# The norms of two products: a root with one Newton step, two column pairs at once, no adding DMA

## The chip, the cores and the metric

One core of one Trainium2 chip. The time is the device time of one execution in microseconds; the profile is of one execution, recorded by the hardware profiler. PE is TensorE's matmuls, PEld its weight loads, DVE is VectorE, ACT ScalarE, POOL GpSimd, SP the engine that only issues transfers.

## The reference

Two networks behind each other on an activation of 256 positions by 1024 channels, all in f32. The first block, with `T = 256` positions:

```
u = rms_norm(h, norm_mix_pre);  proj = u @ w_in            # 1024 x 6656
four branches of width 256 (LRU, pooling, HGRN, short conv), each @ its w_branch, gated, summed = merged
h = h + rms_norm(merged @ w_out, norm_mix_post)            # 1024 x 1024
u = rms_norm(h, norm_mlp_pre);  hid = relu(u @ w_up)**2    # 1024 x 4096
h = h + rms_norm(hid @ w_down, norm_mlp_post)              # 4096 x 1024
rms_norm(x, g) = x * rsqrt(mean(x*x) + 1e-6) * g
```

The second block has two layers. Each is a gated feed-forward net (`ffn1`: norm, 1024 x 5632, silu(a)*b, 2816 x 1024), a mixer (projections `qkv`, `glu`, `gat`; q and k normalised and turned with rope tables; windowed attention, a convolution of 31 taps, products `att`, `cpr` and `out`), a second such net (`ffn2`) and a norm. The output is the activation after both layers.

## The kernel before

The activation stands transposed: channels on the 128 partitions, 256 positions along the free dimension, so a product of 1024 inputs has eight input slices `k`, and its outputs come in column pairs of 256 channels, one PSUM bank per pair (three banks `mm` take turns). For f32 accuracy each weight block (128 x 2048, 1 MB) and each input is split into a high part (`hi`, a ScalarE cast to the matmul's type) and a low part (`lo`, the weight less its high part, on VectorE), and each pair is the sum of three products per slice and half: high by high, high by low, low by high; 48 matmuls for a pair of eight slices.

`weights` (line 159) serves the blocks in a planned order, `ahead` blocks before their use: SP issues the transfer into one of two `raw` buffers, ScalarE casts `hi`, VectorE subtracts `lo`; `hi` and `lo` have three buffers each. Where the plan says `how=1`, ScalarE writes the block's negative, rounded to the matmul's type, into `lo` instead (line 180), and a transfer of POOL's queue adds the block from memory to it as it lands (line 181); the plan of block 1 does this for pairs 1 and 3 of `wout` (line 746).

The order of the instructions of each engine is set before the run by a scheduler: among what is ready by its own model, it takes what the program wrote first; `high_priority(offset=300)` counts its instructions as if written 300 earlier, and `issue_after(ins)` puts what it holds behind `ins` on that engine. So a position in the code is not a position in a queue.

`post` (line 922) does `w_out` and `w_down` with their norms. Over four pairs, each result is squared (ScalarE) and added up, and scaled by its gain into `post`. For the last pair, TensorE adds the squares over the channels with a column of ones (`colsum`, line 258; 256 sums, two columns of 128), VectorE makes the inverse root of these 128 x 2 numbers in eleven steps (`rsqrt`, line 241: affine, a first guess by the bits, three Newton steps of three), and TensorE spreads it over the partitions (`bcast`, line 282). Then, pair by pair, VectorE multiplies and adds to the residual (lines 948 and 949), and `norm.feed` (line 328) splits the new activation, scaled by the next norm's gain, into the next product's inputs `xs` (cast on ScalarE, line 301; low part on VectorE, line 302). The next norm's own factor is applied after the next product (`norm.done`, line 348), so that product can start with the first slice. `post` holds the weights back: in its last pair only one block is fetched ahead (`hold`), and the low part of the block after that is put behind the last feed (`issue_after`).

The next product after `w_out` is `wup` (line 909), that after `w_down` is `ffn1` of layer 0 (lines 370 and 376): pair by pair with `mm` (line 225).

The mixer (line 409) begins with two rope tables per layer: SP issues a small transfer `qkg` (line 425) and POOL makes eight products of it (line 430). They depend on nothing else than free tiles.

## Time and profile before

| | us |
|---|---|
| median of three runs (lowest, highest) | 1859.76 (1857.1, 1862.05) |
| the profiled execution | 1860.85 |
| its span, first to last instruction | 1859.1 |
| PE busy in it | 1789.8 |
| DVE busy | 1329.3 |
| ACT busy | 922.5 |
| POOL busy | 45.1 |

The mean granted clock of TensorE is 0.987 of its full speed. A busy time tells how long an engine had an instruction in work, not that it was at its best; the time that can be had is where TensorE waits or where its clock is low. The span is that of the profiled execution; the time of an execution is some 1.75 us longer than its span.

### The profile page before, as it was taken

The numbers are of one execution on the slowest core, as the hardware profiler recorded it, in microseconds if no ns is written. First come the engines' busy times: TensorE is split into PE (matmuls) and PEld (weight loads), VectorE is DVE, ScalarE is ACT, GpSimd is POOL, SyncE is SP. The second block draws the span as 40 slices with busy tenths as digits, with TensorE's granted clock in tenths as the row PEclk, the third lists the DMA queues.
The fourth block names the chain that finished last, engine by engine and source line by source line (L and its number), as shares of the span: only waits on it lengthen the run. The fifth ranks groups of instructions, "written<-read, shape, count | busy, mean of one in ns | idle before, by whom it ended". The sixth has DMA issues, their size and how long they took to land.

```text
span 1859.1 us, 32925 instructions
## 1 busy us (share of the span) xinstructions
PE 1789.8 (96%) x14048; PEld 1708.5 (92%) x14048; DVE 1329.3 (72%) x2047; ACT 922.5 (50%) x1036; POOL 45.1 (2%) x71
## 2 busy tenths in 40 slices
PE   8999989998999999989999999999999989999997
PEld 7989989997999997778999999999997778999997
DVE  7985777545765698888776656765599888776653
ACT  4354544333544455566654445444454566654442
POOL 0000000000000000000010000000000000000000
PEclk9999989999999999999999999999999999999999
DMA  7526645553555568886355555555569886355552
GB/s 284 175 98 204 186 149 188 182 182 122 204 182 185 179 205 268 235 249 181 129 198 182 182 180 183 182 182 193 180 197 267 257 237 181 128 191 182 184 185 85
DMA packets 53858, 350.57 MB, mean 189 GB/s; under 512 B 6224, under 2 KB 6352, under 8 KB 14288
## 3 DMA queue, kind: packets, MB, share of 16 engines
q1 hardware_dynamic: 47664, 309.44, 47.0%
q0 software_dynamic: 5184, 37.75, 10.7%
q8 instruction: 110, 1.80, 0.4%
q10 hardware_dynamic: 864, 1.28, 0.2%
q14 instruction: 36, 0.29, 0.0%
HBM read 347.40 MB, written 1.05 MB: 187 GB/s over the span
## 4 chain that ended last, share of the span: by engine, by line
PE 66%; issue 14%; DMA 10%; DVE 6%; ACT 4%; POOL 0%; ACTq 0%; DVEq 0%; POOLq 0%
PE mm L222 60%; DMA raw<-qkv 7%; ACT hi L182 3%; DMA raw<-gat 2%; DVE lo L184 2%; PE y L552 1%; PE tr L544 1%; PE pc L264 1%; PE pc L274 1%; PE sc L527 1%; DMA raw<-out 1%; DMA lo<-wout 0%; PE pb L286 0%; DVE spare L589 0%; PE sc L531 0%
## 5 line engine op out<-in xcount | busy, mean ns | idle before, releaser
L222 PE MATMUL mm<-xs,hi 128*128 128x256 f32 x5568 | 1003.7, 284 | 10.5 <-ACT hi L173 5.9
L222 PEld LDWEIGHTS mm<-xs,hi 128*128 128x128 f32 x5568 | 853.1, 190 | 18.7 <-ACT hi L173 5.9
L184 DVE TENSOR_TENSOR lo<-raw,hi 128x2048 fp32r<-128x2048 f32 (+1 forms) x252 | 569.2, 2259 | 308.2 <-ACT hi L182 307.8
L222 PE MATMUL mm<-xs,lo 128*128 128x256 f32 x2784 | 761.9, 284 | 11.0 <-DVE lo L184 5.7
L182 ACT CAST hi<-raw 128x2048 fp32r<-128x2048 f32 (+1 forms) x288 | 542.4, 1885 | 445.7 <-PE mm L222 360.6
L222 PEld LDWEIGHTS mm<-xs,lo 128*128 128x128 f32 x2784 | 516.6, 190 | 15.7 <-DVE lo L184 6.7
L222 PE MATMUL mm<-slot,hi 128*128 128x256 f32 x2304 | 405.1, 281 | 2.9 <-DVE slot L299 1.5
L222 PEld LDWEIGHTS mm<-slot,hi 128*128 128x128 f32 x2304 | 348.1, 188 | 3.7 <-DVE slot L299 2.0
L222 PE MATMUL mm<-slot,lo 128*128 128x256 f32 x1152 | 309.3, 281 | 0.0
L222 PEld LDWEIGHTS mm<-slot,lo 128*128 128x128 f32 x1152 | 210.9, 188 | 0.0
L589 DVE SCALAR_TENSOR_TENSOR slot<-slot,prm,slot 128x256 f32<-128x256 f32 x360 | 149.2, 480 | 0.0
L298 ACT CAST slot<-f 128x256 fp32r<-128x256 f32 (+1 forms) x104 | 45.2, 438 | 193.1 <-DVE f L385 192.0
L469 PE MATMUL mm<-lo,xs 128*128 128x512 f32 x288 | 118.2, 410 | 15.2 <-DMA lo<-qkv 15.1
L470 PE MATMUL mm<-hi,xs 128*128 128x512 f32 x288 | 116.6, 405 | 0.0
L468 PE MATMUL mm<-hi,xs 128*128 128x512 f32 x288 | 115.9, 403 | 0.0
L180 ACT ACTIVATE lo<-raw 128x2048 fp32r<-128x2048 f32 x36 | 68.8, 1912 | 92.2 <-DMA raw<-qkv 58.3
L469 PEld LDWEIGHTS mm<-lo,xs 128*128 128x128 f32 x288 | 55.1, 191 | 33.5 <-DMA lo<-qkv 21.2
L299 DVE TENSOR_TENSOR slot<-f,slot 128x256 fp32r<-128x256 f32 (+1 forms) x104 | 48.0, 465 | 38.0 <-ACT slot L298 38.0
L381 DVE TENSOR_TENSOR z<-mm,rb 128x512 f32<-128x512 f32 x88 | 60.6, 691 | 14.9 <-PE mm L222 13.1
L468 PEld LDWEIGHTS mm<-hi,xs 128*128 128x128 f32 x288 | 55.3, 192 | 13.1
L470 PEld LDWEIGHTS mm<-hi,xs 128*128 128x128 f32 x288 | 55.2, 192 | 12.5
L589 DVE SCALAR_TENSOR_TENSOR spare<-slot,prm,spare 128x256 f32<-128x256 f32 x120 | 49.8, 472 | 0.0
(259 smaller groups left out, 1238.9 us busy)
## 6 DMA issues: line engine op xcount, KB each, us to landing
raw<-ffn1u SPq DMA_DIRECT2D x44, 1024.0 KB, 4.8
raw<-ffn2u SPq DMA_DIRECT2D x44, 1024.0 KB, 4.8
raw<-qkv SPq DMA_DIRECT2D x36, 1024.0 KB, 6.8
raw<-win SPq DMA_DIRECT2D x24, 1024.0 KB, 4.8
lo<-qkv POOLq DMA_DIRECT2D x18, 1024.0 KB, 9.1
raw<-wup SPq DMA_DIRECT2D x16, 1024.0 KB, 4.8
raw<-wdown SPq DMA_DIRECT2D x16, 1024.0 KB, 4.7
raw<-ffn1d SPq DMA_DIRECT2D x16, 1024.0 KB, 4.9
```

Source lines behind the costliest of these rows:

```text
L180: nc.scalar.mul(lo[:, :w], r[:, :w], -1.0)
L182: nc.scalar.copy(h[:, :w], r[:, :w])
L184: nc.vector.tensor_sub(lo[:, :w], r[:, :w], h[:, :w].bitcast(F32))
L222: nc.tensor.matmul(pt[:, m], w[:, i, c], x[k], start=first and m == 0 and i == 0 and j == 0, stop=last and i == n - 1 and j == 2, skip_gro ...
L264: self.nc.tensor.matmul(pc[:, t:t + 1], x[:, t * P:(t + 1) * P], self.ones[:, :1], start=first and t + i == 0, stop=last and i == len(tile ...
L298: nc.scalar.copy(H, src)
L299: return nc.vector.tensor_sub(L, src, H.bitcast(F32))
L381: nc.vector.tensor_mul(z, pt, norm.rb2)
L468: nc.tensor.matmul(pz[j], H[k][:, js], h[:, w], start=k == 0, stop=False)
L469: nc.tensor.matmul(pz[j], H[k][:, js], lo[:, w], start=False, stop=False)
L470: nc.tensor.matmul(pz[j], L[k][:, js], h[:, w], start=False, stop=k == 7)
L589: nc.vector.scalar_tensor_tensor(acc[i], u, w, acc[i], op0=ALU.mult, op1=ALU.add)
```

## The change

In `post`, the norm's factor comes from `rsqrt1`: ScalarE takes the square root of the mean square plus epsilon (a bias that stands in a tile of its own, 16 columns wide, of which one is used), VectorE its reciprocal, and one Newton step in three instructions follows. A square root of something at hand (`root`) is taken ahead of the last pair's square. The square and the sums of the last pair are done in two halves. The next product's first two pairs, in `wup` and in `ffn1` of layer 0, run side by side in `mm_duo`: slice by slice, both pairs' high-by-high, high-by-low and the first pair's low-by-high, and at the end the second pair's low-by-high. The hold and the ordered issue of weights in `post` are dropped. `wout` has no adding transfers. The small transfer `qkg` is issued by ScalarE, behind the fifth silu of the last net before (`ffn1` of its layer).

```diff
--- before.py
+++ after.py
@@ -148,6 +148,9 @@
         nc = self.nc
         self.ones = self.con.tile([P, P], F32, name="ones")
         nc.vector.memset(self.ones, 1.0)
+        self.eps = self.con.tile([P, 16], F32, name="eps")
+        nc.vector.memset(self.eps, EPS)
+        self.eps = self.eps[:, :1]
         self.ident = self.con.tile([P, P], F32, name="ident")
         self.X = [self.st.tile([P, 2, NT], F32, name=f"x{j}") for j in range(4)]
 
@@ -232,6 +235,30 @@
             self.mm_pair(pt, h, lo, H, L, range(k0, k0 + n), k0 == 0, k0 + n == nk)
         return pt
 
+    def mm_duo(self, name, j, H, L):
+
+        nc = self.nc
+        pts = [self.p_mm.tile([P, 2, NT], F32, name="mm") for _ in range(2)]
+        ws = [self.weights(name, j + e) for e in range(2)]
+        ops = [(e, w, x, k) for k in range(KD) for e, w, x in ((0, 0, 0), (1, 0, 0), (0, 0, 1), (1, 0, 1), (0, 1, 0))]
+        ops += [(1, 1, 0, k) for k in range(KD)]
+        for e, w, x, k in ops:
+            wt = ws[e][w].rearrange("p (k n) -> p k n", n=256)
+            for m in range(2):
+                nc.tensor.matmul(pts[e][:, m], wt[:, k, m * P:(m + 1) * P], (H, L)[x][k],
+                                 start=k == 0 and w == x == m == 0, stop=k == KD - 1 and w == 1,
+                                 skip_group_check=True)
+        return pts
+
+    def mms(self, name, n, H, L, duo):
+
+        m = 0
+        if duo:
+            yield from enumerate(self.mm_duo(name, 0, H, L))
+            m = 2
+        for j in range(m, n):
+            yield j, self.mm(name, j, KD, H, L)
+
     def plan_pairs(self, name, npair, nk, dma=()):
         for j in range(npair):
             for k0 in range(0, nk, 8):
@@ -253,6 +280,21 @@
             y2 = keep if keep is not None and it == 2 else y
             nc.vector.scalar_tensor_tensor(y2, a, 1.5, y, op0=ALU.add, op1=ALU.mult)
             y = y2
+        return y
+
+    def rsqrt1(self, src, n, scale, eps=EPS):
+
+        nc = self.nc
+        s = self.small(n, "ns")
+        nc.scalar.activation(s, src, AF.Sqrt, scale=scale, bias=self.eps)
+        v = self.small(n, "nv")
+        nc.vector.tensor_scalar(v, src, scale, eps, op0=ALU.mult, op1=ALU.add)
+        y = self.small(n, "ny")
+        nc.vector.reciprocal(y, s)
+        a = self.small(n, "na")
+        nc.vector.tensor_mul(a, y, y)
+        nc.vector.scalar_tensor_tensor(a, a, -0.5, v, op0=ALU.mult, op1=ALU.mult)
+        nc.vector.scalar_tensor_tensor(y, a, 1.5, y, op0=ALU.add, op1=ALU.mult)
         return y
 
     def colsum(self, tiles, pc=None, first=True, last=True):
@@ -367,20 +409,21 @@
             self.rb2 = self.rb[:, None, :].to_broadcast([P, 2, NT])
 
 
-    def ffn(self, l, n, norm, after):
+    def ffn(self, l, n, norm, after, duo=False):
         nc = self.nc
         nk = DFF2 // P
         hid = [self.slot(i, [P, 4, NT], F32R) for i in range((nk + 1) // 2)]
         H = [hid[k // 2][:, k % 2] for k in range(nk)]
         L = [hid[k // 2][:, 2 + k % 2] for k in range(nk)]
-        for m in range(nk):
-            pt = self.mm(f"{n}u{l}", m, KD, norm.H, norm.L)
+        for m, pt in self.mms(f"{n}u{l}", nk, norm.H, norm.L, duo):
             if m == 0:
                 norm.done()
             z = self.t2("z")
             nc.vector.tensor_mul(z, pt, norm.rb2)
             s = self.t1("s")
-            nc.scalar.activation(s, z[:, 0], AF.Silu)
+            ins = nc.scalar.activation(s, z[:, 0], AF.Silu)
+            if m == 4:
+                self.mark = ins.ins
             f = self.t1("f")
             nc.vector.tensor_mul(f, s, z[:, 1])
             self.split(f, H[m], L[m])
@@ -422,7 +465,8 @@
             self.U[i] = u
 
         qkg = self.slot(13, [P, 6, 2, HD])
-        nc.sync.dma_start(qkg.rearrange("p a b c -> p (a b c)"), self.d[f"qkg{l}"].to_broadcast([P, 768]))
+        with self.tc.issue_after(self.mark):
+            nc.scalar.dma_start(qkg.rearrange("p a b c -> p (a b c)"), self.d[f"qkg{l}"].to_broadcast([P, 768]))
         rts = [self.slot(14 + kind, [P, 3, 2, 2, HD]) for kind in range(2)]
         for kind in range(2):
             for b in range(2):
@@ -648,7 +692,7 @@
         nc = self.nc
         for l in range(NL):
             nx = self.Norm(self, f"mix_norm{l}")
-            self.ffn(l, "ffn1", norm, nx.feed)
+            self.ffn(l, "ffn1", norm, nx.feed, l == 0)
             nx2 = self.Norm(self, f"ffn2_norm{l}")
             self.mixer(l, nx, nx2.feed)
             if l + 1 < NL:
@@ -743,7 +787,7 @@
             self.plan("win", j)
         for k in BORDER:
             self.plan("wbr", k)
-        self.plan_pairs("wout", 4, KD, (1, 3))
+        self.plan_pairs("wout", 4, KD)
         self.plan_pairs("wup", 16, KD)
         self.plan_pairs("wdown", 4, DFF // P)
 
@@ -906,8 +950,7 @@
         hid = [self.slot(j, [P, 4, NT], F32R) for j in range(16)]
         HH = [hid[k // 2][:, k % 2] for k in range(32)]
         HL = [hid[k // 2][:, 2 + k % 2] for k in range(32)]
-        for j in range(16):
-            pt = self.mm("wup", j, KD, nx.H, nx.L)
+        for j, pt in self.mms("wup", 16, nx.H, nx.L, True):
             if j == 0:
                 nx.done()
             z = self.t2("z")
@@ -924,33 +967,34 @@
         nc, tc = self.nc, self.tc
         acc = None
         ms = []
-        pc = None
         for j in range(4):
             if j == 3:
                 pc = self.colsum([acc[:, 0], acc[:, 1]], last=False)
-            pt = self.mm(name, j, nk, H, L, j == 3)
+            pt = self.mm(name, j, nk, H, L)
             with tc.high_priority(offset=300):
+                m = self.tp.tile([P, 2, NT], F32, name="post", tag="zq", bufs=6)
                 if j == 3:
+                    root = self.small(1, "root")
+                    nc.scalar.activation(root, acc[:, 0, :1], AF.Sqrt)
                     sq = self.t2("sq")
-                    nc.scalar.square(sq, pt)
-                    pc = self.colsum([sq[:, 0], sq[:, 1]], pc, first=False)
+                    nc.scalar.square(sq[:, 0], pt[:, 0])
+                    pc = self.colsum([sq[:, 0]], pc, first=False, last=False)
+                    nc.scalar.square(sq[:, 1], pt[:, 1])
+                    pc = self.colsum([sq[:, 1]], pc, first=False)
+                    r = self.rsqrt1(pc, 2, 1.0 / D)
                 else:
                     acc = self.sumsq(acc, pt)
-                m = self.tp.tile([P, 2, NT], F32, name="post", tag="zq", bufs=6)
                 for i in range(2):
                     nc.scalar.mul(m[:, i], pt[:, i], self.prm(gain, 2 * j + i))
                 ms.append(m)
         with tc.high_priority(offset=300):
-            rb = self.bcast(self.rsqrt(pc, 2, 1.0 / D))
+            rb = self.bcast(r)
             for j in range(4):
                 for c in (slice(0, 1), slice(1, 2)) if j == 0 else (slice(0, 2),):
                     m = ms[j][:, c]
-                    ins = nc.vector.tensor_mul(m, m, rb[:, None, :].to_broadcast(list(m.shape)))
+                    nc.vector.tensor_mul(m, m, rb[:, None, :].to_broadcast(list(m.shape)))
                     nc.vector.tensor_add(self.X[j][:, c], self.X[j][:, c], m)
-                ins = norm.feed(j, False)
-        self.ahead = 2
-        with tc.issue_after(ins.ins):
-            self.weights(name, 3, (nk - 1) // 8 * CH)
+                norm.feed(j, False)
         norm.sums()
 
     def finish(self, k, y, slot, YS):
```

## Rows read from the trace of the kernel before

**Rows 1.** The page: busy us (share of the span) and instructions of each engine.

```profile
PE 1789.8 (96%) x14048; PEld 1708.5 (92%) x14048; DVE 1329.3 (72%) x2047; ACT 922.5 (50%) x1036; POOL 45.1 (2%) x71
```

**Rows 2.** Stretches: length, busy of PE, PEld, DVE, ACT, POOL, granted clock, DMA.

```profile
190.00:217.00 27.00, 23.84 (x197) 23.20 (x195) 25.89 (x36) 13.38 (x13) 1.01 (x1) 1.00 0.61 182
218.97:222.38 3.41, 3.41 (x19) 3.41 (x18) 1.40 (x1) 0.00 (x0) 0.00 (x0) 0.50 0.30 53
242.94:253.06 10.12, 7.18 (x31) 6.84 (x32) 8.57 (x23) 4.70 (x11) 0.00 (x0) 0.50 0.00 0
264.00:413.00 149.00, 149.00 (x1262) 149.00 (x1260) 94.25 (x77) 62.05 (x52) 0.00 (x0) 1.00 0.54 188
440.93:447.67 6.74, 4.19 (x17) 3.85 (x18) 5.26 (x15) 2.66 (x6) 0.08 (x1) 0.50 0.00 0
```

**Rows 3.** Timeline (start, us, instruction, [idle before <-releaser]), start of `wout`.

```profile
211.19 2.28 DVE L299 TENSOR_TENSOR xs<-slot,xs 128x256 fp32r<-128x256 f32 x4
215.97 2.21 DVE L299 TENSOR_TENSOR xs<-slot,xs 128x256 fp32r<-128x256 f32 x4
217.52 0.39 PE L222 MATMUL mm<-xs,lo 128*128 128x256 f32 x1 [2.45 <-DMA lo<-wout]
```

**Rows 4.** Groups by line, each shape apart: busy us, mean ns, idle before.

```profile
L184 DVE TENSOR_TENSOR lo<-raw,hi 128x2048 fp32r<-128x2048 f32 x236 | 541.0, 2292 | 294.4 <-ACT hi L182 294.0
L554 DVE RECIPROCAL rec<-den 128x8 f32<-128x8 f32 x4 | 0.8, 198 | 0.0
L596 ACT ACTIVATE mb<-pc 128x256 f32<-128x256 f32 x2 | 0.8, 385 | 0.0
L851 ACT ACTIVATE lb<-lb 128x2 f32<-128x2 f32 x1 | 0.2, 199 | 0.0
L1026 ACT ACT_TABLE_LOAD x1 | 1.3, 1283 | 0.0
```

**Rows 5.** Timeline of TensorE after boundary 1.

```profile
248.24 0.41 PE L222 MATMUL mm<-xs,lo 128*128 128x256 f32 x1
248.88 0.41 PE L222 MATMUL mm<-xs,lo 128*128 128x256 f32 x1
```

**Rows 6.** Timeline at boundary 1, ScalarE and TensorE.

```profile
240.15 0.60 ACT L935 ACTIVATE sq<-mm 128x512 f32<-128x512 f32 x1 [3.02 <-PE mm L222]
240.80 1.05 PE L264 MATMUL pc<-ones,sq 128*128 128x1 f32 x8 [0.69 <-ACT sq L935]
244.16 1.19 PE L286 MATMUL pb<-ident,ny 128*128 128x128 f32 x4 [2.31 <-DVE ny L254]
247.07 0.58 PE L222 MATMUL mm<-xs,hi 128*128 128x256 f32 x1 [1.72 <-ACT xs L301]
```

**Rows 7.** Timeline at boundary 2.

```profile
436.58 4.43 POOL L430 TENSOR_TENSOR slot<-slot,rope 128x192 f32<-128x192 f32 x8 [6.33 <-DMA slot<-qkg]
438.32 0.52 DVE L252 SCALAR_TENSOR_TENSOR na<-na,nv 128x2 f32<-128x2 f32 x1
441.76 1.19 PE L286 MATMUL pb<-ident,ny 128*128 128x128 f32 x4 [4.34 <-DVE ny L254]
```

**Rows 8.** Timeline of TensorE behind both boundaries; waits of its weight loads, 444 to 456.

```profile
257.25 0.39 PE L222 MATMUL mm<-xs,lo 128*128 128x256 f32 x1 [0.99 <-DVE lo L184]
454.86 0.38 PE L222 MATMUL mm<-xs,lo 128*128 128x256 f32 x1 [1.34 <-DVE lo L184]
...
PEld mm L222 <- DVE xs L302: 0.6, 2, 0.3
```

**Rows 9.** Timeline of ScalarE, the casts of the feed behind boundary 1.

```profile
248.84 0.91 ACT L301 ACTIVATE xs<-x,prm 128x256 fp32r<-128x256 f32 x2 [0.90 <-DVE x L949]
250.90 0.91 ACT L301 ACTIVATE xs<-x,prm 128x256 fp32r<-128x256 f32 x2 [0.64 <-DVE x L949]
```

**Rows 10.** Timeline in layer 0's last product.

```profile
936.80 4.68 POOL L430 TENSOR_TENSOR slot<-slot,rope 128x192 f32<-128x192 f32 x4 [17.49 <-DVE slot L638]
941.82 0.38 PE L222 MATMUL mm<-slot,hi 128*128 128x256 f32 x1 [1.52 <-DVE slot L299]
```

## Prediction

> **What bounds the kernel now.** I read the engine shares first: TensorE is busy for 1789.8 of 1859.1 us and VectorE for 72% [rows 1]. So time can only come from places where TensorE stands still or runs slowly, and the next view is a table of stretches, with the granted clock. In a plain stretch (264 to 413) it does 1262 matmuls in 149 us, 0.118 us each, with no idle time. Around the two normalised products it does not: it is idle for part of 190 to 217 although VectorE is 96% busy there (25.89 of 27.00 us), and in three stretches (218.97 to 222.38, 242.94 to 253.06, 440.93 to 447.67) the granted clock is 0.50, the lower of its two levels, 1.2 instead of 2.4 GHz [rows 2]. The timeline then names the waits. I call the restart after `wout` (240 us) boundary 1 and that after `wdown` (436 us) boundary 2.
>
> **The change part by part.**
>
> *A. No adding DMA in `wout`.* TensorE waits 2.45 us, until 217.52, for the adding DMA that finishes the low half of pair 1 [rows 3]. That goes. In its place VectorE must subtract: 2.29 us [rows 4], in a stretch in which it is free for 1.1 us of 27 [rows 2]. The subtraction becomes ready near 208 us, ahead of the two groups of four that write the product's inputs (211.19 and 215.97 [rows 3]). If it goes first, the first group moves from 211.2 to 213.5, TensorE, which has matmuls of the step before until 211.7, starts the product at some 213.4, 1.7 us late (the cast on ScalarE runs just ahead of each subtraction), and no longer waits for a DMA: 2.45 - 1.7 = 0.7 us gained. If it goes between the groups, TensorE starts on time and waits until 215.8: 1.7 us gained. If the merges are held up in full and more splitting follows, 1 us is lost. I take 0.7, since there [rows 3] VectorE runs without a gap. Pair 3's DMA makes TensorE wait for nothing, and its subtraction falls after 222 us, where VectorE has one such subtraction to make per pair, 2.29 us in the 48 x 0.118 = 5.7 us that TensorE takes for it; without that cover it would cost its 2.29. After the old wait the clock is low for 3.41 us [rows 2]. At that level it is 0.64 us from one low-half matmul to the next, three matmuls on (248.24 to 248.88), 0.213 each [rows 5], so 1 - 0.118 / 0.213 = 45% of such a stretch is lost, here 1.5 us. With a shorter pause it may not fall; I take half, 0.75, with 0 and 1.5 as ends. A: 1.45.
>
> *B. The norm's chain.* Boundary 1: the product ends at 240.11 (the sums start at 240.80, after a wait of 0.69 for the square), the sums take 1.05, TensorE then waits 2.31 for VectorE's eleven steps (0.21 each, hand-overs included), and the broadcast starts at 244.16: 4.05 us after the product [rows 6]. New: the first half-square starts at the same time (+0.04), the second some 0.36 later, and takes about 0.39 (a 128x256 ScalarE read of PSUM [rows 4]), so it ends at +0.79; its half of the sums starts 0.05 later and takes 0.53, to +1.37; ScalarE's root of 128x2 takes 0.20 [rows 4] with a hand-over of 0.04 on either side, to +1.65; a reciprocal and three steps, four times 0.21 (a reciprocal of 128x8 takes 0.198 [rows 4]), and the broadcast starts at +2.49. Gain 1.56. The first affine step runs on VectorE beside the root, the two scalings of the last pair on ScalarE beside the sums. Behind the root, which now makes ScalarE wait for TensorE, stands the cast of pair 2's weights; it is late by some 0.6 us, and TensorE needs it only after the first two pairs. Boundary 2: TensorE waits 4.34 us before its broadcast at 441.76; with the same 1.05 and 0.69 ahead of that the product ended at 435.68, 6.08 us before. POOL multiplies the rope tables from 436.58 for 4.43 us, and VectorE's steps take 0.52 meanwhile [rows 7], against 0.21 with their hand-over at boundary 1. These multiplications move behind the fifth silu of `ffn1`, where neither engine is on the path; so the same chain gives 6.08 - 2.49 = 3.59. If the POOL work stayed, about 2 us of that would not come. B: 5.15.
>
> The dummy root ahead of the last pair's square has the table load moved off the chain: a load takes 1.28 us [rows 4], and ScalarE is idle for 3.02 us before the square at 240.15 [rows 6], so it is hidden; uncovered it costs 1.28 once. (The Trainium skill, "ScalarE: Activation LUTs", Table sets: the hidden batching unit, speaks against this change: work is to be grouped by table set, and each change of set costs about 2.66 us with its drain, against the 1.28 shown. By it the load still ends before the square, and the sum is the same; what it would do if square and root did not share a set is a rival below.)
>
> *C. Two pairs side by side.* TensorE now waits for the low half of the second pair 0.99 us at 257.25 and 1.34 us at 454.86, and 0.6 us for inputs [rows 8]. Without the hold the second pair's low half is made before the product ends, on an idle VectorE, and its use comes last of 96 matmuls. Ten matmuls per input slice take 1.18 us; the inputs come one per 1.03 us (ScalarE's casts, two slices each, start 2.06 apart, at 248.84 and 250.90 [rows 9]). So nothing starves: 0.99 + 1.34 + 0.6 = 2.9 us. The cost hidden behind it: the first two pairs' weights are let go together, so pair 3's subtraction starts late; I count it as nothing (it has all of pair 2, 48 x 0.118 = 5.7 us) with an end of 1 us lost per boundary.
>
> *D. The clock.* Matmuls run at the low level from 247.07 to 253.06 and, with the same 2.91 from broadcast to first matmul, from 444.67 to 447.67 [rows 2, 6, 7]: 45% of 6.0 and of 3.0, 2.7 and 1.3 us, and both broadcasts with them. The gaps get shorter but stay: 2.49 + 2.91 = 5.4 us from product to next product, against 6.96 and 8.99. I take the mean of the two old losses, 2.0, for each: no change. Ends: both gone (4.0 gained, and half of 1.19 on each broadcast), both as at boundary 1 (1.4 lost).
>
> *E. The rope tables of layer 1.* At 936.80, still in layer 0's mixer, POOL makes the second layer's tables for 4.68 us, and TensorE waits 1.52 us at 941.82 for a VectorE split that this slows [rows 10]; no such wait stands at the same place of layer 1. The tables now wait for layer 1's own `ffn1`. I take 1.4, ends 0 and 1.5. On SP the two small DMAs stood between weight loads that wait for a free buffer anyway, so their leaving gives nothing; ScalarE issues them behind a silu, on a tile that has long been free, with casts and silus behind them for which nobody hurries: nothing, or a few tenths if TensorE's weights were late there. The constant: nothing (a memset at the start, beside the first loads).
>
> Sum: 1.45 + 5.15 + 2.9 + 0 + 1.4 = 10.9 us. The profiled execution took 1860.85 (span 1859.1); less 10.9 it is 1849.95. It lay 1.1 above the median of the three runs, 1859.76, so I forecast a median of **1848.9 us**.
>
> **The rivals.**
> 1. *A split gets into the waits of the chain.* The hold and the ordered issue kept pair 1's subtraction behind the feed, and pair 2's behind that. Without them pair 2's (2.29 us) can start on VectorE in the 1.2 us of the broadcast [rows 6]. For it: VectorE is idle there, and the order is set ahead of the run by what is ready first. Against: the cast that it needs (1.9 us) follows the root and is done hardly sooner than the broadcast. Price about 2 us per boundary: 1853.
> 2. *The root costs a switch of tables on the path.* If square and root had no set in common, each boundary would load twice on the path, 4 x 1.28 = 5.1: 1854. Against: in the groups by line no load stands at the line of a square. (By the 2.66 us that the Trainium skill's "ScalarE: Activation LUTs" gives for a change of set, it would be 10.6, and 1859.5.)
> 3. *Not faster but slower: splits ahead of the norm everywhere.* If ScalarE puts the 1.9 us cast ahead of the true root and VectorE a 2.29 us subtraction ahead of the scaling at both boundaries, each restart comes 4.2 us later, and one more low stretch of 3.4 us costs 1.5 each: 11.4; if the subtraction in `wout` delays the merges in full, A turns from +1.45 to -2.3. Together 15 us: 1864. It decides from about 11 us of such delay. Against: all of the norm's steps are traced in a high-priority block.
> 4. *The clock stays up at both boundaries and in `wout`*: 4.0 + 1.2 + 0.75 more, 1843. For it: the gap of `wout` shrinks. Against: the gaps at the boundaries hold barely 2 us of TensorE work. (The Trainium skill, "TensorE: Matmul & The Clock Gate", Part 1, says that the count of slow matmuls of one kernel changes from run to run; no run here shows that yet.)
> 5. *Nothing of note*: the order of the instructions shifts elsewhere and gives the gain back, 1858.
>
> **How the numbers follow.** Forecast 0.54 (its own range 1846 to 1852), rivals 1 to 5: 0.17, 0.07, 0.06, 0.09, 0.07. The range reaches over rival 1 and 2 and most of 4: 1843.5 to 1856. What a measurement here can tell from no change is 0.3%, 5.6 us, so faster means below 1854.2: the forecast, rival 4, most of rival 1 and a little of 2: 0.74. Same: part of 1, 2 and 5, and the milder half of 3: 0.20. Slower: 0.06.
>
> **What would show it.** No wait for an adding DMA near 217; root, reciprocal and three steps between the sums and a broadcast that starts some 2.5 us after each product; POOL's table work near 490 and 1190; no wait for a low half in the first two pairs after each boundary; the wait at 941 gone. I am wrong if a subtraction of 2048 columns stands between the sums and the first scaling, if a table load stands between square and root, or if the merges before `wout` end over 2 us later.

## The result, and the profile after

The changed kernel takes 1841.37 us (median of four, 1839.62 to 1843.05) where the kernel before takes 1858.88 beside it: a ratio of 0.9893, 95% interval 0.9873 to 0.9914. Timed again later it was 1836.8 against 1862.31, 0.9858 (0.9839 to 0.9877). The forecast, 1848.9, had 10.9 us of gain; 17.5 came in the first comparison and 25.5 in the second.

The first page of the profile, engine line, answers to [rows 1]:

```profile
PE 1774.8 (96%) x14048; PEld 1693.8 (92%) x14048; DVE 1328.8 (72%) x2038; ACT 921.1 (50%) x1041; POOL 45.7 (2%) x69
```

TensorE does the same 14048 matmuls and is *busy* for 15.0 us less. Waits that go away don't lower a busy time; cheaper matmuls do, and less time at the low clock. The stretches show both, beside [rows 2] (columns: window, its length, then busy time and count by engine, granted clock, DMA share, GB/s):

```profile
196.00:219.00 23.00, 19.50 (x155) 18.32 (x154) 22.79 (x34) 10.19 (x11) 0.00 (x0) 1.00 0.39 138
240.10:246.80 6.70, 4.98 (x25) 4.73 (x24) 6.37 (x14) 4.42 (x10) 0.00 (x0) 0.50 0.00 0
264.00:413.00 149.00, 148.44 (x1270) 148.24 (x1271) 92.01 (x76) 62.74 (x53) 0.00 (x0) 1.00 0.53 184
431.30:438.00 6.70, 4.98 (x22) 4.68 (x23) 5.63 (x13) 4.03 (x8) 0.00 (x0) 0.50 0.00 0
```

In 264 to 413, where no matmul was edited and the clock is 1.00 in both, 1270 matmuls fit in 148.44 us where 1262 took 149. The stretch of low clock near 219 is gone, that at boundary 1 is 6.7 instead of 10.1 us, that at boundary 2 as long as it was. The waits of TensorE around both restarts, from the timeline (start, duration, operation, in brackets the idle time before it and its releaser), beside [rows 3, 6 to 8]:

```profile
209.68 0.50 PE L225 MATMUL mm<-slot,hi 128*128 128x256 f32 x2 [1.13 <-DVE slot L939]
237.30 1.05 PE L306 MATMUL pc<-ones,sq 128*128 128x1 f32 x8 [0.47 <-ACT sq L980]
239.65 0.74 PE L328 MATMUL pb<-ident,ny 128*128 128x128 f32 x4 [1.30 <-DVE ny L297]
242.12 1.22 PE L248 MATMUL mm<-xs,hi 128*128 128x256 f32 x4 [1.72 <-ACT xs L343]
262.67 0.68 PE L328 MATMUL pb<-ident,rs 128*128 128x128 f32 x4 [0.40 <-DVE rs L281]
264.54 0.50 PE L225 MATMUL mm<-xs,hi 128*128 128x256 f32 x2 [1.19 <-DVE z L957]
...
428.86 1.05 PE L306 MATMUL pc<-ones,sq 128*128 128x1 f32 x8 [0.47 <-ACT sq L980]
431.21 1.12 PE L328 MATMUL pb<-ident,ny 128*128 128x128 f32 x4 [1.30 <-DVE ny L297]
434.06 1.22 PE L248 MATMUL mm<-xs,hi 128*128 128x256 f32 x4 [1.72 <-ACT xs L343]
454.37 0.68 PE L328 MATMUL pb<-ident,rs 128*128 128x128 f32 x4 [0.39 <-DVE rs L281]
456.24 0.51 PE L225 MATMUL mm<-xs,hi 128*128 128x256 f32 x2 [1.19 <-DVE z L422]
```

From a product's end to the broadcast it is now 0.47 + 1.05 + 1.30 = 2.82 us at both boundaries (4.05 and 6.08 before; forecast 2.49). No matmul waits for a low half of the first two pairs any more. But some 20 us behind each restart stand two waits that weren't there, 0.4 and 1.2 us, for the *next* norm. VectorE's timeline shows what is late:

```profile
258.91 0.16 DVE L279 SCALAR_TENSOR_TENSOR na<-na,nv 128x2 f32<-128x2 f32 x1
258.99 2.29 DVE L187 TENSOR_TENSOR lo<-raw,hi 128x2048 fp32r<-128x2048 f32 x1
261.20 0.15 DVE L281 SCALAR_TENSOR_TENSOR ny<-na,ny 128x2 f32<-128x2 f32 x1
```

A weight subtraction stands in the middle of that norm's eleven steps, so its factor, the first scaled results `z` and the PSUM bank that they free are 2.2 us later.

To see where the 18.2 us between the two first profiles (spans 1859.1 and 1840.9) went, I compared the starts of the same matmuls in both, by their number in TensorE's order. "Spacing" is the part from plain spacings of successive matmuls (105 to 126 ns in both, 12,070 of them: 118.05 ns on average before, 116.88 after), "rest" is waits and clock:

| stretch (us in before) | gain | spacing | rest | forecast |
|---|---|---|---|---|
| start to `w_out` (to 209) | 1.98 | 1.54 | 0.44 | 0 |
| `w_out` (209 to 234) | 1.43 | 0.20 | 1.23 | A 1.45 |
| boundary 1 (234 to 277) | 1.77 | 0.32 | 1.45 | B, C 2.6 |
| plain (277 to 430) | 2.11 | 2.12 | 0.0 | 0 |
| boundary 2 (430 to 479) | 3.75 | 0.16 | 3.59 | B, C 5.5 |
| plain (479 to 680) | 1.20 | 1.25 | 0.0 | 0 |
| mixer of layer 0 (to 930) | -0.54 | 0.69 | -1.23 | 0 |
| 930 to 950 | 1.44 | 0.08 | 1.36 | E 1.4 |
| the rest | 5.03 | 7.72 | -2.69 | 0 |

14.1 of 18.2 us are the spacing of matmuls, which the forecast nowhere touched; in the mixers and behind them some of it is lost again to waits and clock (the negative rests).

### The profile page after: what moved, and what is told of

It is laid out like the page before. It is cut to its first block, busy times and chain, and to the rows that moved or that the text cites. A ratio compares the mean times of both kernels' runs of the same rounds, so it can differ in the third digit from the quotient of the medians.

```text
span 1840.9 us, 32917 instructions
## 1 busy us (share of the span) xinstructions
PE 1774.8 (96%) x14048; PEld 1693.8 (92%) x14048; DVE 1328.8 (72%) x2038; ACT 921.1 (50%) x1041; POOL 45.7 (2%) x69
## 3 DMA queue, kind: packets, MB, share of 16 engines
HBM read 345.30 MB, written 1.05 MB: 188 GB/s over the span
## 4 chain that ended last, share of the span: by engine, by line
PE 68%; DMA 10%; DVE 10%; ACT 5%; issue 4%; POOL 0%; ACTq 0%; DVEq 0%; POOLq 0%
PE mm L225 60%; DMA raw<-qkv 5%; DVE lo L187 4%; ACT hi L185 3%; DMA raw<-gat 2%; PE y L596 1%; DMA lo<-qkv 1%; PE mm L248 1%; PE tr L588 1%; PE pc L316 1%; PE pc L306 1%; PE sc L571 1%; DMA raw<-win 1%; DMA raw<-out 1%; PE mm L513 0%
## 5 line engine op out<-in xcount | busy, mean ns | idle before, releaser
L225 PE MATMUL mm<-xs,hi 128*128 128x256 f32 x5440 | 967.8, 282 | 10.6 <-ACT hi L176 5.9
L225 PEld LDWEIGHTS mm<-xs,hi 128*128 128x128 f32 x5440 | 825.9, 189 | 18.4 <-ACT hi L176 5.9
L225 PE MATMUL mm<-xs,lo 128*128 128x256 f32 x2720 | 739.1, 282 | 7.4 <-DVE lo L187 3.7
L225 PEld LDWEIGHTS mm<-xs,lo 128*128 128x128 f32 x2720 | 501.6, 189 | 11.6 <-DVE lo L187 4.5
L183 ACT ACTIVATE lo<-raw 128x2048 fp32r<-128x2048 f32 x34 | 65.0, 1912 | 79.5 <-DMA raw<-qkv 55.2
```

Of the source, the lines that this page charges most:

```text
L183: nc.scalar.mul(lo[:, :w], r[:, :w], -1.0)
L225: nc.tensor.matmul(pt[:, m], w[:, i, c], x[k], start=first and m == 0 and i == 0 and j == 0, stop=last and i == n - 1 and j == 2, skip_gro ...
```

## The experiments

The only thing in the change that reaches every product is where the data lie: the constant's tile (16 columns, 64 bytes) stands ahead of most of what is allocated behind it, so the inputs `xs`, the residual, the slots (the buffers that hold the inputs of the other products) and the small tiles lie 64 bytes further on; the weights (`raw`, `hi`, `lo`) stay. **Theory: the place of a matmul's moving input sets the plain pace. Rival: the change itself gives the gain.**

**p1**, the kernel before with this tile and nothing else:

```diff
+        self.eps = self.con.tile([P, 16], F32, name="eps")
+        nc.vector.memset(self.eps, EPS)
```


> The kernel before with one thing added: the tile of 16 columns for epsilon and the instruction that fills it, which nothing reads. Every tile behind it (identity, parameters, activations, product inputs, temporaries) lies 64 bytes higher; weights do not move. In the profiles a matmul of the plain stretches takes 118.3 ns before and 116.7 to 117.8 after, 12.9 us over the whole execution, in stretches whose code did not change. Theory 'place': that comes from the 64 bytes; this kernel takes 1859 - 13 = 1846 us (1843 to 1849), and its plain stretches show the pace of after. Theory 'rest of the change': the pace comes with another part or differs from execution to execution; this kernel takes 1859 +- 2.5, with 118.3 ns.

1853.36 us against 1866.59 beside it, ratio 0.9931 (0.9909 to 0.9954), mean spacing 116.61 ns. A tile that nobody reads makes the kernel 13 us faster, with the same mean granted clock, 0.985, in its runs and in those of before beside them. (Its profile is 10.6 us shorter than the first one of before: the spacings give 17.3, of which waits and clock take 6.6 back.)

**p2**, the change with the constant in a spare column of a tile that the allocation holds anyway:

```diff
-        self.eps = self.con.tile([P, 16], F32, name="eps")
...
-        warm = b.con.tile([P, 1], F32, name="warm")
...
+        warm = b.con.tile([P, 2], F32, name="warm")
...
+        b.eps = warm[:, 1:]
...
```


> The changed kernel, with epsilon kept in the spare bytes of a tile that was there before, so that all tiles lie where they lay before the change. Theory 'place': the pace goes back to 118.3 ns a matmul and 13 us are lost: 1841 + 13 = 1854 us (1851 to 1857). Theory 'rest of the change': 1841 +- 2.5, with the pace of after.

1853.39 us, ratio 0.9934 (0.9913 to 0.9956), spacing 118.04 as before. Its profile is 5.4 to 7.0 us shorter than the two profiles of before (spans 1852.1 against 1857.5 and 1859.1); the ratio says 12, with an interval from 8 to 16. The granted clock goes with it: the ten runs of before beside it, 1860.4 to 1869.7 us, have 0.985 on average and p2's six have 0.989, while the two profiled runs of before had 0.987 and 0.990. So the change proper is worth some 5 to 12 us, place about as much again.

**p3**, before with another tile widened, 32 bytes:

```diff
-        warm = b.con.tile([P, 1], F32, name="warm")
...
+        warm = b.con.tile([P, 16], F32, name="warm")
...
```


> The kernel before with the small tile that warms ScalarE made 16 columns wide, so that the activations, product inputs and temporaries lie 32 bytes higher and begin on a multiple of 64 bytes (before and after they begin 32 past one); parameters and weights stay. Theory 'place': the pace changes again; if it is the multiple of 64 that counts, this is at least as fast as 1846 us, and if it is only the distance to the weights, anything from 1846 to 1859. Theory 'rest of the change': 1859 +- 2.5, 118.3 ns.

1879.83 us, ratio 1.0078 (1.0051 to 1.0105), spacing 119.59. Slower was in none of my readings: place works in both directions.

**p4** and, later, **e3**: the change again.

> The changed kernel as it is, profiled once more. Theory 'place' (and any theory by which the program sets the pace): the same pace in the same stretches, 117.8 ns up to 134 us, 116.7 ns from 134 to 440, 117.8 from 449 to 950, 116.7 from 955 to 1330, 117.8 from 1600 on. If the pace is a matter of the single execution, these stretches lie elsewhere.

> The change, unchanged, timed on the same chip as the version with the split behind the norm: 1840 to 1843 us, ratio 0.9893 again, and the waits of 0.4 and 1.2 us behind both restarts as in its two other profiles. If the waits differ, they belong to the execution and not to the program.

1839.99 (one run), and 1836.8 with ratio 0.9858, below what I expected of e3; p1's and p2's ratios multiplied are 0.9866. The spacings are 116.58 and 116.67. But the paces do not stand in the same stretches, as I had expected of p4: 590 to 625 has 303 matmuls in p4 and e3 and 299 in the first profile, 350 to 400 has 427 in e3 and 431 in the other two. At this place a stretch has one of two paces, and which one differs between executions; the mean is below that of before each time. In e3 the low stretch at boundary 1 was 3.4 us, in p4 6.8. The late waits stand in both profiles at both boundaries (in e3 0.35 and 1.19 us at 262.91 and 264.78, 0.45 and 1.19 at 456.17 and 458.04), so they belong to the program.

**c1**, before again:

> The kernel before, unchanged, profiled on the chip that gave it 1866.6 us as a median of ten. Theory place: its plain matmuls are 0.1183 us apart here too (1160 in the 137 us from 267 to 404, as in the first profile), and whatever makes it 7 us longer than the 1859.8 of before is in TensorE's clock or its waits. Rival (the pace belongs to the chip or the execution, not to the program): another pace here, near 0.119, and the ratios of the runs beside it are to be read anew.

1859.24, spacing 118.04, as in the first profile of before: at that place the pace is the program's. **c2**, before with an unread tile ahead of the slots only:

```diff
+        pad = self.ar.tile([P, 16], F32, name="pad")
+        nc.vector.memset(pad, 0.0)
```


> The kernel before with one unread tile of 16 columns at the start of the pool of the slots: the slots and the small tiles lie 64 bytes further on, the inputs xs, the residual x and the rope tables stay. Theory: what counts is where a matmul's own moving input lies. Then w_up, glu and the other products that read xs keep 0.1183 us per matmul, w_down and the down products, which read slots, come to 0.1167 to 0.1178 (1160 to 1175 matmuls in the 137 us of w_down where before has 1160), and the whole is some 4 us faster than before. Rival: what counts is where VectorE and ScalarE read and write beside TensorE, so that all products change alike or none does.

The stretches, c1 first and c2 below it; 280 to 320 lies in `wup`, whose matmuls read `xs`, 350 to 400 in `wdown`, whose matmuls read slots (PE alone: window, length, busy time and count, clock, DMA share, GB/s; a count includes the few already in work at the start):

```profile
280.00:320.00 40.00, 40.00 (x340) 1.00 0.55 184
350.00:400.00 50.00, 50.00 (x425) 1.00 0.53 186
```

```profile
280.00:320.00 40.00, 40.00 (x340) 1.00 0.53 184
350.00:400.00 50.00, 50.00 (x431) 1.00 0.54 188
```

Only the product whose own inputs moved got faster. 1857.1 us in one run, 2 us less than c1 where I had expected 4: by the table's method the spacings give 5.2, and waits and clock take 3.0 back (mean granted clock 0.984, c1 0.990).

To find the order of the places took four more runs: **d2** (moved by 96; its edit stands with the change's own steps below), and **e2**, **f1** and **f2**, which are before with an unread tile of 32, 64 and 48 columns; the edit of e2:

```diff
+        self.eps = self.con.tile([P, 32], F32, name="eps")
+        nc.vector.memset(self.eps, EPS)
```


> The kernel before with an unread tile of 32 columns: activations, slots and small tiles 128 bytes further on (inputs at 96 mod 128 bytes again, at 224 instead of 96 mod 256). Theory: the pace goes by the place mod 128: plain matmuls 0.1183 us apart as in before, 1160 in the 137 us of 267 to 404, and a time of before, 1858 to 1866. Rival: the pace goes by another period or by the distance from something that doesn't move: another pace, as in the runs moved by 32, 64 and 96 (0.1200, 0.1166, 0.1169).

> The kernel before with an unread tile of 64 columns: all behind it 256 bytes further on, inputs at 96 mod 256 bytes as in before. The theory of a period of 128 fell (moved by 128: 0.1200 and not 0.1183). Theory now: the period is 256 bytes, so this is before again: 0.1183 us per plain matmul, a span of 1857 to 1866 us. Rival: it is no period but the distance from something that stays (the weights), and another pace comes again, 0.1167 or 0.1200.

> The kernel before, all behind the unread tile of 48 columns moved by 192 bytes, inputs at 32 mod 256 bytes (the change has them at 160, 0.1166 to 0.1169 on average). Theory with a period of 256: a sixth value that none of the five tells; with the steps seen (0.1180 at 96, 0.1196 at 128, 0.1166 at 160, 0.1169 at 192, 0.1196 at 224) all I can say is that it lies in 0.1166 to 0.1200. If it is 0.1166 to 0.1169, the residues 32 mod 128 go together; if 0.1196 to 0.1200, the order has no use that I can name.

The same stretch of `wdown`, in p3, p1, d2, e2, f2 and f1, that is moved by 32, 64, 96, 128, 192 and 256 bytes:

```profile
350.00:400.00 50.00, 50.00 (x419) 1.00 0.50 170
```

```profile
350.00:400.00 50.00, 50.00 (x431) 1.00 0.54 188
```

```profile
350.00:400.00 50.00, 50.00 (x427) 1.00 0.53 187
```

```profile
350.00:400.00 50.00, 50.00 (x419) 1.00 0.50 174
```

```profile
350.00:400.00 50.00, 50.00 (x424) 1.00 0.54 187
```

```profile
350.00:400.00 50.00, 50.00 (x425) 1.00 0.54 190
```

| moved by (bytes) | inputs start at (bytes, mod 256) | mean plain spacing, ns |
|---|---|---|
| 0 (before, c1), 256 (f1) | 96 | 118.05, 118.04; 118.06 |
| 32 (p3) | 128 | 119.59 |
| 64 (p1, the change three times) | 160 | 116.61; 116.88, 116.58, 116.67 |
| 96 (d2, without the duo) | 192 | 116.91 |
| 128 (e2) | 224 | 119.62 |
| 192 (f2) | 32 | 117.87 |

My period of 128 bytes fell with e2 (119.62 and not 118.0; 1869.43 us in one run); one of 256 agrees with f1 (1859.45 us in one run) and has no other test here. f2 (1860.41 in one run) came at 117.87, between, so 32 and 160 don't go together. No rule for the order shows, and the means hide some of it: d2 has 355 matmuls in 1200 to 1240, the change at 64 has 345 there, although d2 is slower than it in `wdown`. The weights stand still in all these runs, so the place of the inputs can't be told from their distance to the weights.

**The change's own steps.** The base is p2 (nothing moved), since its spacing is that of before. **c3**, without the two pairs side by side; **d1**, the same done to the change as it is; **d2**, d1 with the constant's tile 24 columns wide:

```diff
-        for j, pt in self.mms("wup", 16, nx.H, nx.L, True):
+        for j, pt in self.mms("wup", 16, nx.H, nx.L, False):
...
-            self.ffn(l, "ffn1", norm, nx.feed, l == 0)
+            self.ffn(l, "ffn1", norm, nx.feed, False)
```


> The change with nothing moved in memory, without the two pairs side by side (both products after the norms go pair by pair, the hold stays away). Reference: the change with nothing moved, 1853.4 us, ratio 0.9934. My forecast had 2.9 us for the duo: then 1856.3, ratio 0.995, and the wait for a low half is back in both restarts (0.99 and 1.34 us before). Rival: the duo gives nothing net, because behind it TensorE now waits 0.3 and 1.2 us at 266 and 268 and as much at 460 and 462 for the next norm, split by weight subtractions: then 1853.4 or less and those four waits are gone.

> The change as it is (constant in its own tile, all behind it moved by 64 bytes) without the two pairs side by side. Theory: place and duo are independent. The duo's removal gave 0.9905 in place of 0.9934 where nothing was moved, place alone 0.9931: so 0.9893 minus 0.003 is 0.986 (the change itself with the duo's loss taken out), and by the product of place and the other version 0.984; plain matmuls 0.1167 to 0.1178 us apart, no wait of 1.2 us for z behind either restart. Rival: the duo's loss was luck of the clock in one profile and the ratio stays at 0.989.

> The same with the constant's tile 24 columns wide, so that all behind it lies 96 bytes further on than before (inputs begin at 64 mod 128 bytes; they stood at 96 in before, 0.1183 us per matmul; at 0 in the run moved by 32, 0.1200; at 32 in the change, 0.1167 to 0.1178). Theory: the pace goes by the place mod 128, and 64 is a fourth value, which I put between its neighbours 32 and 96, near 0.1175: ratio 0.986 to 0.988. Rival: it goes by mod 64, so 64 is as 0: 0.1200 and some 25 us more than the other version, ratio near 0.999.

c3 1845.17 us, ratio 0.9905 (0.9883 to 0.9927), against p2's 1853.39: the rival that I had put beside it, with no wait for the next norm. In the column "rest" of the table boundary 1 gains 3.1 and boundary 2 6.1 us on the first profile of before, where p2 gains 1.3 and 3.25: the duo costs 1.8 and 2.8. About 1 us of the 2.8 is clock: the low stretch there is 3.4 us in c3 and 6.8 in p2. Where the rest of the difference in time lies isn't shown. d1 1832.08, ratio 0.9846 (0.9829 to 0.9863), the fastest of all. d2 1837.96, 0.9873 (0.9853 to 0.9892): 64 bytes are the better place for this version too, if anything, but the intervals overlap.

**e1**, the change with only the order of the one subtraction set (the fifth pair's, behind the first `z`):

```diff
-                nc.vector.tensor_sub(lo[:, :w], r[:, :w], h[:, :w].bitcast(F32))
+                with self.tc.issue_after(self.behind) if self.behind else ExitStack():
+                    nc.vector.tensor_sub(lo[:, :w], r[:, :w], h[:, :w].bitcast(F32))
...
+            self.behind = self.z0 if duo and j == m else None
```


> The change as it is, with one thing put in order: the low half of the fifth pair of weights after each restart stands behind the first scaled result z on VectorE, and so no longer between the eleven steps of the next norm (it stood there, 2.29 us, at 262.41 and 450.69 in the runs of the change). Theory: the duo loses because of that split: TensorE's waits of 0.4 us (broadcast) and 1.2 us (z) at both restarts go, 3.2 us in all, and with them most of the 4 us that the versions without the duo gained there; ratio 0.987 to 0.988 against the change's 0.9893. Rival: the duo loses by letting its weights go late, so that the next splits come late whatever their order; then TensorE waits for a low half instead and the ratio stays at 0.989 or above, while without the duo it was 0.9846.

VectorE in e1, at the end of the next norm's steps:

```profile
262.35 0.16 DVE L286 SCALAR_TENSOR_TENSOR rs<-na,ny 128x2 f32<-128x2 f32 x1
263.94 0.69 DVE L964 TENSOR_TENSOR z<-mm,rb 128x512 f32<-128x512 f32 x1 [1.42 <-ACT rb L339]
264.55 2.28 DVE L189 TENSOR_TENSOR lo<-raw,hi 128x2048 fp32r<-128x2048 f32 x1
```

The steps run through, and TensorE's waits behind both restarts are gone. The boundaries gain 3.1 and 5.4 us on before in the column "rest" (e3 beside it 2.2, with a low stretch of only 3.4 us, and 3.3), about what they gain without the duo (3.1 and 6.1 in c3). So with the duo this one split makes the loss, and the duo itself is worth nothing measurable. As a time, 1835.49 (0.986, 0.9843 to 0.9876), it can't be told from e3's 1836.8.

But such a split costs nothing by itself. VectorE in c3 has one between the steps too, and another behind them, ahead of the first `z`:

```profile
258.79 2.29 DVE L184 TENSOR_TENSOR lo<-raw,hi 128x2048 fp32r<-128x2048 f32 x1
261.27 2.29 DVE L184 TENSOR_TENSOR lo<-raw,hi 128x2048 fp32r<-128x2048 f32 x1
```

TensorE waits for neither. There the next norm's sums start 12.2 us behind the restart (256.16 less 244.01), in p2 14.7 (259.76 less 245.11). So the duo loses by two things together: it makes the next norm 2.5 us later, and it lets both weights go at once (ScalarE casts the two that follow in one go from 257.59 in p2, but at 256.00 and at 258.43 in c3), so that one subtraction stands ahead of the late steps and one between them.

**c4**, the old eleven steps, one square and one set of sums in p2:

```diff
...
-                    r = self.rsqrt1(pc, 2, 1.0 / D)
...
+                    r = self.rsqrt(pc, 2, 1.0 / D)
...
```


> The change with nothing moved in memory, but with the norm's factor by the eleven steps on VectorE, one square of the last pair and one set of sums, as before; no root. Reference 1853.4, ratio 0.9934. My forecast had 1.56 us for the chain at each boundary beside what the rope tables cost the second: then 4.05 us again from the product's end to the broadcast at both (2.8 with the new chain), 2.5 us longer in all from 1.25 each, 1855.9, ratio 0.995. Rival: the clock takes back what the shorter gap gives or adds to it (low stretches of 10 us instead of 7 at the boundaries), 1.5 us more each: 1859, ratio 0.9965.

1853.94 us, ratio 0.9961 (0.9941 to 0.9982), which can't be told from p2's 0.9934 as a time. In the profile the chain is 4.05 us again (0.69, 1.05 and 2.31), 1.23 more, and the low stretch at boundary 1 is some 10 us long again. And the restart after it is worse than in before:

```profile
242.09 0.16 DVE L278 SCALAR_TENSOR_TENSOR ny<-na,ny 128x2 f32<-128x2 f32 x1
242.17 2.29 DVE L184 TENSOR_TENSOR lo<-raw,hi 128x2048 fp32r<-128x2048 f32 x1
244.38 0.75 DVE L988 TENSOR_TENSOR post<-post,pb 128x256 f32<-128x256 f32 x2
```

This is my rival 1 to the letter: a split between the last step and the first scaling, and the first matmul 3.65 us after the broadcast starts instead of 2.91 (246.05 less 242.40; [rows 6]). The same stands at boundary 2 (at 438.28). It comes with the long chain and not with the short one: in the change the cast that the split needs ends at 240.8 (it starts at 238.91 and takes 1.90), when the first scaling has started (240.44).

**d3**, the adding DMAs of `w_out` back; **d4**, the rope tables' transfers on the sync queue again:

```diff
-        self.plan_pairs("wout", 4, KD)
+        self.plan_pairs("wout", 4, KD, (1, 3))
```

```diff
-        with self.tc.issue_after(self.mark):
-            nc.scalar.dma_start(qkg.rearrange("p a b c -> p (a b c)"), self.d[f"qkg{l}"].to_broadcast([P, 768]))
+        if True:
+            nc.sync.dma_start(qkg.rearrange("p a b c -> p (a b c)"), self.d[f"qkg{l}"].to_broadcast([P, 768]))
```


> The change with nothing moved, but the pairs 1 and 3 of w_out get their low halves by the adding DMA again. Reference: the change with nothing moved, ratio 0.9934. My forecast had 1.45 us for taking it out (0.7 of the wait, 0.75 of the clock). Theory: the waits of 2.6 us (pair 1) and, in the second profile of before, 2.05 us (pair 3) come back, the merges' own waits (1.34) go, so 2 to 4 us longer: ratio 0.9945 to 0.9955. Rival: those DMA waits are hidden by what ends last anyway (the merges of VectorE): same ratio, 0.9934.

> The change with nothing moved, but the small transfers for the rope tables stand on the sync queue again, behind nothing. Then POOL makes the tables again beside the second norm (436 us) and in the mixer of layer 0 (near 937). Theory of my forecast: 2 us longer at the second restart if the new short chain is slowed as the old one was (its last steps on VectorE took 0.52 in place of 0.21 us), 1.4 us longer near 941: 3.4 us, ratio 0.9953. Rival: the new chain has only four steps behind the root, so POOL costs it 1.2 us at most, and what the change gains there comes from the chain alone: ratio 0.9945 or less.

d3 1852.71 (0.995, 0.9933 to 0.9968), d4 1852.97 (0.9953, 0.9937 to 0.997): as times neither differs from p2. In the profiles both steps show. d3's wait is back:

```profile
219.24 0.39 PE L222 MATMUL mm<-xs,lo 128*128 128x256 f32 x1 [2.40 <-DMA lo<-wout]
```

and `w_out` gains 0.37 us on c1 where p2 gains 1.66: A is worth 1.3. d4's chain at boundary 2, TensorE and then VectorE:

```profile
438.93 1.20 PE L325 MATMUL pb<-ident,ny 128*128 128x128 f32 x4 [2.35 <-DVE ny L294]
```

```profile
436.92 0.16 DVE L288 TENSOR_SCALAR nv<-pc 128x2 f32<-128x2 f32 x1 [3.26 <-ACT ns L286]
437.00 0.15 DVE L290 RECIPROCAL ny<-ns 128x2 f32<-128x2 f32 x1
437.18 0.51 DVE L292 TENSOR_TENSOR na<-ny 128x2 f32<-128x2 f32 x1
437.73 0.52 DVE L293 SCALAR_TENSOR_TENSOR na<-na,nv 128x2 f32<-128x2 f32 x1
438.27 0.51 DVE L294 SCALAR_TENSOR_TENSOR ny<-na,ny 128x2 f32<-128x2 f32 x1
```

2.35 instead of 1.30: with the tables beside it the short chain pays 1.05 us, the rival's "1.2 at most", not my 2. Steps with two inputs in SBUF go from 0.16 us (in the change) to 0.51, the one with a single input there and the one that reads `pc`, in PSUM, stay. (The Trainium skill, "GPSIMD Engine Reference", 1. Specifications, says that GpSimd and VectorE share an interface to SBUF and contend when VectorE has two SBUF inputs; these rows agree.) Near 934 TensorE waits 0.66 us in d4 and 0.29 in p2; in before it was 1.52 [rows 10].

## Why the prediction was wrong

**The step that failed: "The constant: nothing (a memset at the start, beside the first loads)."** I priced the instruction and not the room: 64 bytes in front of most tiles. Measured alone (p1) it is ratio 0.9931, 13 us; in the first profiles 14.1 us of spacing. My row for it was there ([rows 2], 0.118 us per plain matmul), but I took that for the price of such a matmul, when it was the price of one at this place. The low end of my range, 1843.5, which left this term out, is 2 us above the result.

*A* was right in size (forecast 1.45, measured 1.2 to 1.7), but not in its parts. The subtraction went ahead of the last merges; TensorE waits 1.13 us for one of these at 209.68 and another 1.0 in three short waits for its inputs, up to 216.30, where I had counted 1.7. So this wait gives 0.3 and not 0.7, and the rest goes with the clock: six of the nine profiles with the adding DMA have a low stretch of 3.4 us near 219, none of the ten without it. Where there is none, pair 3's DMA can cost instead, which I had at nothing: in c1 TensorE waits 1.77 us for it at 233.39.

*B* came as written: root, reciprocal and three steps, 1.23 us saved at boundary 1 (forecast 1.56) and 3.26 at boundary 2 (3.59). Both are 0.33 short: the sums end 1.52 us after the product where I had 1.37, and the broadcast starts 1.30 later where I had 1.12. The table load is hidden, here on ScalarE, which is otherwise idle:

```profile
233.22 1.28 ACT L978 ACT_TABLE_LOAD   x1
234.51 0.20 ACT L978 ACTIVATE root<-sqa 128x1 f32<-128x1 f32 x1
```

The square (236.87) comes after it, and no load stands between square and root at either boundary: rival 2 is out.

*C*, forecast 2.9, came to nothing: p2's boundaries gain 1.3 and 3.25, which is B alone. The waits for low halves go, but without the duo they are gone too: c3 shows the boundaries at 3.1 and 6.1 us, the sums of B and C as I forecast them being 2.6 and 5.5. Of the steps that order the weights c3 keeps only the dropped hold; that this took the waits away is argued and not shown, since no run puts the hold back alone. The duo takes back 1.8 and 2.8 us, by the late norm and the two subtractions described at e1. I had named the weights that are let go together and counted them as nothing, with an end of 1 us: I looked for the cost at the matmuls of pair 3 and not at the chain queued beside it on VectorE. Rival 1 had the mechanism and the wrong chain.

*D*, forecast as nothing, was something. In the profiles one low stretch at boundary 1 is 3.4 us shorter, 45% of which is 1.5; boundary 2 as before. In the timed runs the mean granted clock is 0.985 for before and 0.989 for p2 beside it, by the same 45% up to 7.5 us (an estimate: a low stretch in which TensorE waits costs less). In the first comparison the change's four runs had only 0.987. It is 0.989 to 0.991 in c3, c4, d3 and d4 too and 0.985 in p1 and p3, so neither place nor any one of the steps that those four take back makes it alone. Part of it can be seen: 10 to 15 us behind the first restart six of the eight profiles of before (moved or not) have a further low stretch, behind the second four of them, and none of the eleven profiles of the change's versions. The dropped hold is the step that no run puts back; whether it makes the difference is open. (The Trainium skill, "TensorE: Matmul & The Clock Gate", Part 1, says that the number of slow matmuls differs between runs of one kernel; the 6.8 us of p4 and the 3.4 of e3 at boundary 1 agree.)

*E*: 1.36 of 1.4 in the profile, though d4 gives back only some 0.4 of it near 934.

Without place the forecast of 10.9 us stands against 4.1 (first profiles), 5.4 to 7.0 (p2's profile against the two of before) and 12 (8 to 16) in p2's times. In the profiles it was over by C's 2.9 and by B's 0.7. That p2's times come near 10.9 all the same is luck: the clock, which I had at nothing, may have given what C did not. The rest of the scatter lies in the two mixers, where two profiles of the same kernel (before and c1) differ by 2.7 us in layer 0: before has three low stretches of 3.4 us there, near 700, 755 and 816, c1 only one near 806. What sets these I haven't tried.

## What to carry to other kernels

Before a change is credited with a gain, put its new tiles where they move nothing, or move everything without the change: in this kernel, where TensorE is busy 96% of the time, a shift of 32 bytes cost 0.8% and one of 64 bytes gave 0.7%, as much as all that the edit did. Look at the spacing of plain matmuls in a stretch that nobody edited; if it differs, the place of the inputs has to be matched first. And when the order of weights is changed, ask for every short chain on the engine that splits them what can now get between its steps, the next norm's chain too, and whether anyone waits for that chain.

## What was not expected of the hardware

The pace of identical matmuls (128 x 256, moving input and weights in SBUF, clock 1.00) goes with the byte address of their moving input (the weights stayed where they were): 119.6 ns on average with inputs at 128 or 224 mod 256, 118.05 at 96, 117.9 at 32, 116.9 at 192, 116.6 to 116.9 at 160. It follows the input's own address product by product (c2). At 160 one stretch can have either of two values in different profiles of the same kernel (427 or 431 matmuls in 350 to 400), and the one profile at 192 has two (342 matmuls in 500 to 540, 355 in 1200 to 1240); what sets these is open, as is the rule behind the order.
